# One shared ring of four PSUM banks, and a convolution gate computed in place, in a two-layer hybrid decoder trunk

## The chip, the cores and the metric

The kernel runs on one core of a Trainium2 chip. The metric is the device time of one execution in microseconds (us), the median of several runs. TensorE (PE) multiplies matrices into PSUM; its weight loads (PEld) overlap its matmuls. VectorE (DVE) and ScalarE (ACT) read PSUM and write SBUF, GpSimd (POOL) works on SBUF, and SyncE (SP) issues the DMAs.

## The reference, cut to what matters

There are two layers over 512 tokens of width 1024. Each layer normalises x to h, projects h to the inputs of four mixers and of a gate, and multiplies the mixers' outputs by the gate, projects them back, normalises and adds:

```python
h = rms_norm(x, pre_norm_g[l])
u = h @ w_in[l]                       # mla | sb | moba | conv | gate
o_a = mla_attention(...)              # causal softmax, 4 heads
o_b = stick_breaking_attention(...)   # sigmoids and a running product, 4 heads
o_c = moba_attention(...)             # softmax with a position bias, 4 heads
a, g = split(u_conv)
xg = a * sigmoid(g)                   # 256 channels
y = depthwise causal convolution of xg, 31 taps, + bias
o_d = silu(layer_norm(y)) @ pw_w + pw_b
y = concat(o_a, o_b, o_c, o_d) * silu(u_gate)
x = x + rms_norm(y @ w_out[l], post_norm_g[l])
```

## The kernel before

The instruction order is written by a planner that runs while the kernel is built. Every piece of work is a generator, a task with a priority (`spawn(priority, task)`; a smaller number goes first). A task yields an engine, an estimated duration and the time from which its inputs are there. `run()` keeps an estimated clock for each engine and lets the task go next whose estimated start, plus a weight times its priority, is smallest. Each engine then executes its instructions in that fixed order; what the planner misjudges shows on the chip as a wait. A change of a buffer therefore makes a new plan for the whole program.

Buffers come from rings. `take(tag, ...)` takes a free buffer of a ring or suspends the task until one is given back with `drop`; tasks that wait for the same ring are asked in the order of their priorities. PSUM has eight banks: `acc` 3, `sc` 2 (scores), `tr` 2 (transposes), `pv` 1. Of the SBUF rings, `zb` has two buffers of 513 columns and `cx` two of 542.

- **Filler** (`filler`, priority 300). The projections of h in the order vC, cg, ca, g0, m0, m1, g2, b0, g3, b1, vB, g1, then the output projection. `feat_chunk` (matmuls at L647) makes 2 x 24 matmuls of 128x512 for a chunk of 256 columns; each 24 fill one `acc` bank, which an `evac` task empties with ACT and DVE. Chunk m0 holds q and k of the first two moba heads (`qk_chunk`, evacuation at L809 and L814), g0 to g3 the gate (`gate_chunk`, L840 and L842).
- **Convolution.** `cg_chunk` takes both `zb` buffers and writes sigmoid(g) into them (ACT, L857). `ca_chunk` takes the two `cx` buffers, clears their first 30 columns (POOL, L868) and multiplies a from PSUM by the gate from `zb` into the rest (DVE, L876), which frees `zb`. `taps` then runs 31 DVE instructions for each 128 channels (L895, L899), which accumulate in an `acc` bank that is held for all 31. `conv_norm` comes after.
- **Attention.** For each of 12 heads four `unit_task`s (128 queries each): scores into `sc` (L1038 or L1043), for softmax a DVE instruction from `sc` into a `zb` buffer (L1070), exp and scaling on ACT (L1078, L1083), transposes into `tr` (L1088), and a split of them into two parts (ACT L376, DVE L382). Stick-breaking units take a `zb` buffer too (L1053). The order of the heads is mla, moba, sb. `pv_task` (priority 12) multiplies by v: eight matmuls into the one `pv` bank (L1104), a copy on ACT (L1111), two additions on DVE (L1117).
- **Weights.** `splitter` casts each weight tile on ACT (L358), `low_part` subtracts on DVE or POOL (L363). `either` is the choice of DVE or POOL for such work; it adds a handicap to DVE, 2000 ns while the convolution's first half runs (`busy`), else 300 ns, and 1500 ns at the very beginning.
- `warm_up` issues matmuls into a PSUM bank before the first input is ready (L441).

Of the kernel before, what the change touches and what calls it, by code (L numbers as in the profile page):

```python
# [13 lines left out]
AF = mybir.ActivationFunctionType  # L14
ALU = mybir.AluOpType
# [4 lines left out]
S = 512  # L20
# [3 lines left out]
DEPTH = 2  # L24
# [6 lines left out]
CW = 31  # L31
# [44 lines left out]
FBS = 1  # L76
SPARE0 = 1500.0
PR = {'low': 155, 'hs': 50, 'lat': 50, 'ev': 50, 'vev': 60, 'va': 65, 'cq': 40, 'q': 35, 'cn': -40, 'pw': -5, 'pv': 12, 'ys': 85, 'ye': 70, 'xn': 20, 'xs': 10, 'bd': 10, 'pre': 70, 'u0': 0, 'u1': 0, 'u2': 21, 'u3': 1}
BANKS = {"acc": 3, "sc": 2, "tr": 2, "pv": 1}
ENGINE = {"dvx": "dve", "plm": "pool"}  # L80
PORT = ("dvx", "pool")
WT = {'pe': 0.078, 'dve': 0.691, 'act': 0.0, 'pool': 0.094, 'sp': 0.496}
# [7 lines left out]
class Flow:  # L90
# [19 lines left out]
    def spawn(self, prio, gen):  # L110
        task = [prio, self.n, gen, None]
        self.n += 1
        self.tasks.append(task)
        self.tasks.sort(key=lambda a: a[:2])
        self.resume(task, None)
# [37 lines left out]
    def wait(self, *names):  # L153
        return (yield lambda: max(self.ev[n] for n in names) if all(n in self.ev for n in names) else None)

    def mark(self, name, t):
        self.ev[name] = t
# [17 lines left out]
    def drop(self, buf, t):  # L175
        buf.at = max(buf.at, t)
        buf.uses -= 1
        if buf.uses == 0:
            self.free[buf.tag].append((buf.at, buf.idx))
            if buf.also:  # L180
                self.drop(buf.also, buf.at)


def pe(n):
    return max(107, 3 + n / 2.255)
# [6 lines left out]
def act(n):  # L192
    return 60 + 0.85 * n
# [6 lines left out]
def dve(n):  # L200
    return 69 + 1.04 * n
# [6 lines left out]
def pool(n):  # L208
    return 150 + 2.1 * n
# [3 lines left out]
def trunk(ctx, tc, x, pre_g, w_in, w_sm, vecs, w_out, post_g, rel_bias, consts, onehot, out):  # L213
    nc = tc.nc
    V, A, G, PE = nc.vector, nc.scalar, nc.gpsimd, nc.tensor
    pEng, aEng, vEng, xEng, gEng, mEng, sEng = "pe", "act", "dve", "dvx", "pool", "plm", "sp"
    fl = Flow()
    spawn, wait, mark, drop = fl.spawn, fl.wait, fl.mark, fl.drop
# [12 lines left out]
    for tag, (_, n) in RING.items():  # L231
        fl.free[tag] = [(0.0, i) for i in range(n)]
    for tag, n in BANKS.items():
        fl.free[tag] = [(0.0, i) for i in range(n)]

    def take(tag, name, n=None, dt=F32, uses=1):
        tag, idx, at = yield from fl.slot(*((tag,) if isinstance(tag, str) else tag))
        if tag in BANKS:
            t = ps.tile([P, 512], F32, name=name, tag=f"{tag}{idx}", bufs=1)
        else:  # L240
            t = ap.tile([P, RING[tag][0]], dt, name=name, tag=f"{tag}_{idx}", bufs=1)
        b = Buf(t if n is None else t[:, :n], tag, idx, at)
        b.uses = uses
        return b
# [68 lines left out]
        return r, t  # L313

    def either(n, t):
        busy = any(("cx", l, 0) in fl.ev and ("ca", l, 0) not in fl.ev for l in range(DEPTH))
        e, t = yield [(xEng, dve(n), t, None, None, SPARE0 if ("h", 0, NT - 1) not in fl.ev else SPARE if busy else 300.0), (gEng, pool(n), t, None, None, 0.0)]
        return (V if e == xEng else G), t

# [41 lines left out]
    def low_part(key, i, raw, r3, h, lo, n, t, b):  # L361
        e, t = yield from either(n, t)
        e.tensor_tensor(lo, r3, h.bitcast(F32), ALU.subtract)  # L363
        drop(raw, t)
        units[key, i] = (h, lo, t, b)
# [4 lines left out]
    def weight(key, k):  # L370
        h, lo, t, b = yield from unit(key, k // 2)
        return h[:, k % 2, :], lo[:, k % 2, :], t, b

    def split(dh, dl, src, n, t, eng=None):
        t = yield aEng, act(n), t
        A.copy(dh, src)  # L376
        if eng is gEng:
            e, t = yield from either(n, t)
            e.tensor_tensor(dl, src, dh.bitcast(F32), ALU.subtract)  # L379
        else:  # L380
            t = yield vEng, dve(n), t
            V.tensor_tensor(dl, src, dh.bitcast(F32), ALU.subtract)  # L382
        return t
# [50 lines left out]

    def warm_up():
        z, t = yield lambda: fl.ev.get("z")
        b = yield from take("pv", "warm")
        zb = z.ap.bitcast(BF16)
        while ("h", 0, 0, 0) not in fl.ev or fl.clock[pEng] < fl.ev["h", 0, 0, 0] - 600:
            te = yield pEng, 107 if t > WARM_AT else 213, t  # L440
            PE.matmul(b.ap[:, :256], zb[:, :P], zb[:, P : P + 256], start=True, stop=True)  # L441
            t = te - LAG
        drop(b, te)
        drop(z, te)
# [190 lines left out]
    def feat_chunk(l, c, evac, pre=None):  # L635
        key = (l, c)
        for m in range(2):
            if pre:
                yield from pre(m)
            a = yield from take("acc", "acc")  # L640
            cs = slice(m * P, (m + 1) * P)
            for k in range(KT):
                th = yield from wait(*[("h", l, t, k // 4) for t in range(NT)])
                wh, wl, tw, b = yield from weight(key, k)
                for i, (w, h) in enumerate(((wh, hs[0]), (wh, hs[1]), (wl, hs[0]))):
                    te = yield pEng, pe(S), max(th, tw, a.at)
                    PE.matmul(a.ap, w[:, cs], h[:, k, :], start=k == 0 and i == 0, stop=k == KT - 1 and i == 2)  # L647
                if m == 1:
                    drop(b, te)
            spawn(PR["ev"], evac(m, a, te))  # L650
# [197 lines left out]
    cx, ca, xn = {}, {}, {}  # L848

    def cg_chunk(l):  # L850
        res = []
        for m in range(2):
            res.append((yield from take("zb", f"cg{m}", S)))

        def evac(m, a, te):
            t = yield aEng, act(S), max(te, res[m].at), "sig"
            A.activation(res[m].ap, a.ap, AF.Sigmoid)  # L857
            drop(a, t)
            mark(("cg", l, m), t)

        cx[l, "g"] = res
        yield from feat_chunk(l, "cg", evac)

    def ca_chunk(l):
        for m in range(2):
            b = cx[l, m] = yield from take("cx", f"cx{m}")
            t = yield mEng, 50, b.at
            G.memset(b.ap[:, : CW - 1], 0.0)  # L868
            b.at = t

        def evac(m, a, te):
            b = cx[l, m]
            tg = yield from wait(("cg", l, m))
            g = cx[l, "g"][m]
            t = yield vEng, dve(S), max(te, tg, b.at)
            V.tensor_tensor(b.ap[:, CW - 1 :], a.ap, g.ap, ALU.mult)  # L876
            drop(a, t)
            drop(g, t)
            mark(("cx", l, m), t)

        yield from feat_chunk(l, "ca", evac)
# [113 lines left out]
    def y_split(l, g, hp, pr, yt, ty):  # L995
        ts = yield from wait(("sg", l, g, hp))
        s = sg[l, g][hp]
        cols = slice(pr * 256, pr * 256 + 256)
        e, t = yield from either(256, max(ts, ty))
        e.tensor_tensor(yt.ap, yt.ap, s.ap[:, cols], ALU.mult)  # L1000
        drop(s, t)
        k = 2 * g + hp
        t = yield from split(ys[0][:, k, cols], ys[1][:, k, cols], yt.ap, 256, t, gEng)
        drop(yt, t)
        mark(("y", l, k, pr), t)
# [89 lines left out]
    def pv_task(l, kind, hp, hh, pt, st, yt):  # L1095
        t0 = yield lambda: max(st.values()) if len(st) == NT else None
        vn = VN[kind]
        tv = yield from wait(*[("v", l, vn, j) for j in range(NT)])
        pv = yield from take("pv", "pv")
        v, v4 = vb[l, vn]  # L1100
        te = yield pEng, 1175, max(t0, tv, pv.at)
        for i, j in PVSEQ:
            lhs = v4[:, j, hp * 2 + hh, : (HD if i else P)]
            PE.matmul(pv.ap[: (HD if i else P), j * P :], lhs, pt[i].ap[:, 4 * j * P : (3 * j + NT) * P],  # L1104
                      start=not i and not j, stop=(i, j) == PVSEQ[-1])
        for b in pt:
            drop(b, te)
        drop(v, te)
        ob = yield from take("ob", "ob")
        t = yield aEng, act(S), max(te, ob.at)  # L1110
        A.copy(ob.ap[:HD, :], pv.ap[HD:, :])  # L1111
        for u in range(2):
            c = slice(u * 256, u * 256 + 256)
            if not hh:
                yt.append((yield from take("yt", "yt")))
            t = yield vEng, dve(256), max(t, yt[u].at)
            V.tensor_tensor(yt[u].ap[hh * HD : (hh + 1) * HD, :], pv.ap[:HD, c], ob.ap[:HD, c], ALU.add)  # L1117
            if hh:
                spawn(PR["ys"], y_split(l, GRP[kind], hp, u, yt[u], t))
        drop(pv, t)  # L1120
        drop(ob, t)
# [239 lines left out]
```

## Time and profile before

| | |
|---|---|
| median of 3 runs | 557.99 us (557.28 to 558.27) |
| the profiled execution | 557.85 us |
| its span, first to last instruction | 555.7 us |
| PE / PEld / DVE / ACT / POOL busy | 536.3 / 460.5 / 421.3 / 367.1 / 186.0 us |
| mean granted TensorE clock | 0.999 |

The profile is of one execution. PE's busy time counts a matmul from its start to its modelled end, and matmuls overlap in the pipeline; so "busy" says that something was under way, and PE's idle time is what is left when nothing was.

### The profile page before, as it was taken

What the parts mean: (1) busy time and instruction counts of PE and PEld (TensorE: products, weight loads), DVE (VectorE), ACT (ScalarE), POOL (GpSimd) and SP (SyncE); (2) the same over time, 40 slices, a digit from 0 to 9 for tenths busy, and PEclk for the clock granted to TensorE, in tenths of its full rate; (3) what the DMA queues carried; (4) which work ended last, traced back from release to release, by engine and by line L of the source; (5) the groups of instructions that cost most, each with busy time, mean ns of one, the idle gap of its engine ahead of it and who ended that gap; (6) DMA issues with size and microseconds to landing.
All of it is one profiled execution on the core that took longest, in us unless ns stands there. A gap on an engine that the chain in (4) does not pass through costs nothing.

```text
span 555.7 us, 9439 instructions
## 1 busy us (share of the span) xinstructions
PE 536.3 (97%) x3181; PEld 460.5 (83%) x3181; DVE 421.3 (76%) x942; ACT 367.1 (66%) x864; POOL 186.0 (33%) x227
## 2 busy tenths in 40 slices
PE   9999999999989999999998999999998999999995
PEld 5997877778868898899998887777876778989995
DVE  4668658999999988953776584999999889697243
ACT  5637568958995746745673665897879558475531
POOL 5733031352224731522332003145323433242321
PEclk9999999999999999999999999999999999999999
DMA  7424233134303163033753214132431322513145
GB/s 279 148 73 140 79 113 97 43 96 128 111 9 114 58 199 105 21 114 128 247 183 99 77 33 138 42 110 67 120 101 58 97 74 60 186 42 96 50 168 181
DMA packets 31026, 59.47 MB, mean 107 GB/s; under 512 B 4034, under 2 KB 5954, under 8 KB 30979
## 3 DMA queue, kind: packets, MB, share of 16 engines
q1 hardware_dynamic: 30978, 58.88, 34.4%
q8 instruction: 25, 0.41, 0.3%
q14 instruction: 23, 0.18, 0.1%
HBM read 49.17 MB, written 5.51 MB: 98 GB/s over the span
## 4 chain that ended last, share of the span: by engine, by line
PE 78%; DVE 10%; ACT 9%; issue 2%; POOL 0%; POOLq 0%; DVEq 0%; ACTq 0%
PE acc L647 31%; PE acc L1132 16%; PE acc L580 7%; PE lat L580 4%; PE pv L1104 4%; PE tr L1088 3%; PE sc L1043 3%; PE sc L1038 2%; ACT p L1083 2%; ACT p L1078 2%; PE acc L710 2%; ACT pt L376 1%; DVE cs L1061 1%; DVE pt L382 1%; PE tr L537 1%
## 5 line engine op out<-in xcount | busy, mean ns | idle before, releaser
L647 PE MATMUL acc<-hH,w 128*128 128x512 f32 x640 | 217.3, 404 | 3.1 <-DVE m L814 1.6
L363 POOL TENSOR_TENSOR w<-raw,w 128x512 fp32r<-128x512 f32 x70 | 94.9, 1361 | 182.1 <-ACT w L358 163.9
L647 PEld LDWEIGHTS acc<-hH,w 128*128 128x128 f32 x640 | 118.5, 188 | 28.2 <-issue 4.0
L647 PE MATMUL acc<-hL,w 128*128 128x512 f32 x320 | 130.0, 406 | 0.0
L358 ACT CAST w<-raw 128x512 fp32r<-128x512 f32 x130 | 79.7, 619 | 44.2 <-PE acc L647 18.3
L899 DVE SCALAR_TENSOR_TENSOR cv<-cx,vec,cv 128x512 f32<-128x512 f32 x116 | 86.6, 747 | 1.2
L1132 PE MATMUL acc<-w,yH 128*128 128x256 f32 x416 | 75.4, 282 | 0.0
L647 PEld LDWEIGHTS acc<-hL,w 128*128 128x128 f32 x320 | 60.3, 188 | 11.5 <-issue 0.9
L363 DVE TENSOR_TENSOR w<-raw,w 128x512 fp32r<-128x512 f32 x60 | 41.4, 697 | 34.6 <-ACT w L358 34.3
L1132 PEld LDWEIGHTS acc<-w,yH 128*128 128x128 f32 x416 | 64.5, 189 | 0.2
L1132 PE MATMUL acc<-w,yL 128*128 128x256 f32 x208 | 58.9, 283 | 0.1
L580 PE MATMUL acc<-w,hH 128*128 128x256 f32 x256 | 49.0, 286 | 0.3 <-DVE w L363 0.3
L382 DVE TENSOR_TENSOR pt<-tr,pt 128x128 fp32r<-128x128 f32 (+3 forms) x96 | 45.8, 483 | 4.0 <-ACT pt L376 3.3
L1088 PE MATMUL tr<-cst,p 128*128 128x128 f32 x240 | 42.5, 275 | 5.8 <-ACT p L1083 5.6
L376 ACT CAST pt<-tr 128x128 fp32r<-128x128 f32 (+3 forms) x96 | 40.3, 423 | 11.3 <-PE tr L1088 10.4
L1088 PEld LDWEIGHTS tr<-cst,p 128*128 128x128 f32 x240 | 29.9, 141 | 19.3 <-ACT p L1083 10.9
L580 PEld LDWEIGHTS acc<-w,hH 128*128 128x128 f32 x256 | 40.3, 189 | 1.1 <-DVE w L363 0.5
L1132 PEld LDWEIGHTS acc<-w,yL 128*128 128x128 f32 x208 | 39.2, 189 | 0.3 <-DVE yL L379 0.3
L580 PE MATMUL acc<-w,hL 128*128 128x256 f32 x128 | 36.2, 283 | 0.0
L1078 ACT ACTIVATE p<-zb,s 128x128 f32<-128x128 f32 (+2 forms) x64 | 35.8, 560 | 0.5 <-ACT p L1083 0.3
L1083 ACT ACTIVATE p<-p,s 128x128 f32<-128x128 f32 (+3 forms) x64 | 35.0, 561 | 0.4 <-DVE s L1081 0.4
L1063 POOL TENSOR_TENSOR p<-p,cs 128x128 f32<-128x128 f32 (+3 forms) x22 | 18.3, 836 | 43.7 <-DVE cs L1061 24.2
(176 smaller groups left out, 1021.9 us busy)
## 6 DMA issues: line engine op xcount, KB each, us to landing
raw<-in_w_in_dram SPq DMA_DIRECT2D x96, 256.0 KB, 2.7
raw<-in_w_out_dram SPq DMA_DIRECT2D x32, 256.0 KB, 2.6
xt<-in_x_dram SPq DMA_DIRECT2D x8, 512.0 KB, 4.1
raw<-in_w_sm_dram SPq DMA_DIRECT2D x8, 256.0 KB, 3.8
bias<-scratch SPq DMA_DIRECT2D x8, 256.0 KB, 3.1
m<-m SPq DMA_DIRECT2D x16, 128.0 KB, 2.2
b<-b SPq DMA_DIRECT2D x16, 128.0 KB, 3.0
x<-xt SPq DMA_DIRECT2D x4, 512.0 KB, 2.9
```

Source lines behind the costliest of these rows:

```text
L358: A.copy(wH, r3)
L363: e.tensor_tensor(lo, r3, h.bitcast(F32), ALU.subtract)
L376: A.copy(dh, src)
L382: V.tensor_tensor(dl, src, dh.bitcast(F32), ALU.subtract)
L580: PE.matmul(o, a[:, k, tc_], w, start=k == 0 and i == 0, stop=k == KT - 1 and i == 2)
L647: PE.matmul(a.ap, w[:, cs], h[:, k, :], start=k == 0 and i == 0, stop=k == KT - 1 and i == 2)
L899: V.scalar_tensor_tensor(o.ap if j == CW - 1 else a.ap, xc[:, j : j + S], vc[:, w0 : w0 + 1], a.ap, ALU.mult, ALU.add)
L1078: A.activation(p.ap[:, :wd], src.ap[:, :wd], AF.Exp, bias=nm[:, 0:1], scale=-1.0, accum_out=ls)
L1083: A.activation(p.ap[:, :wd], p.ap[:, :wd], AF.Copy, scale=r[:, 0:1])
L1088: PE.transpose(tr3[:, j, :], p.ap[:, j * P : (j + 1) * P], ident)
L1104: PE.matmul(pv.ap[: (HD if i else P), j * P :], lhs, pt[i].ap[:, 4 * j * P : (3 * j + NT) * P], start=not i and not j, stop=(i, j) == PVSE ...
L1132: PE.matmul(o, a[:, k, tc_], w, start=first and i == 0, stop=stop and i == 2)
```

## The change

The `pv` bank is given up and `acc` has four banks; `pv_task` and `warm_up` take theirs from `acc`. `cg_chunk` takes the `cx` buffers instead of `zb`, clears their first columns and writes the sigmoid into the rest; `ca_chunk` multiplies in place. `either` keeps the high handicap until the second half of the convolution is done.

```diff
-BANKS = {"acc": 3, "sc": 2, "tr": 2, "pv": 1}
+BANKS = {"acc": 4, "sc": 2, "tr": 2}
@@ either
-        busy = any(("cx", l, 0) in fl.ev and ("ca", l, 0) not in fl.ev for l in range(DEPTH))
+        busy = any(("cx", l, 0) in fl.ev and ("ca", l, 1) not in fl.ev for l in range(DEPTH))
@@ warm_up
-        b = yield from take("pv", "warm")
+        b = yield from take("acc", "warm")
@@ cg_chunk
-        res = []
-        for m in range(2):
-            res.append((yield from take("zb", f"cg{m}", S)))
-
-        def evac(m, a, te):
-            t = yield aEng, act(S), max(te, res[m].at), "sig"
-            A.activation(res[m].ap, a.ap, AF.Sigmoid)
-            drop(a, t)
-            mark(("cg", l, m), t)
-
-        cx[l, "g"] = res
-        yield from feat_chunk(l, "cg", evac)
-
-    def ca_chunk(l):
         for m in range(2):
             b = cx[l, m] = yield from take("cx", f"cx{m}")
             t = yield mEng, 50, b.at
@@
         def evac(m, a, te):
             b = cx[l, m]
+            t = yield aEng, act(S), max(te, b.at), "sig"
+            A.activation(b.ap[:, CW - 1 :], a.ap, AF.Sigmoid)
+            drop(a, t)
+            mark(("cg", l, m), t)
+
+        yield from feat_chunk(l, "cg", evac)
+
+    def ca_chunk(l):
+        def evac(m, a, te):
+            x_ = cx[l, m].ap[:, CW - 1 :]
             tg = yield from wait(("cg", l, m))
-            g = cx[l, "g"][m]
-            t = yield vEng, dve(S), max(te, tg, b.at)
-            V.tensor_tensor(b.ap[:, CW - 1 :], a.ap, g.ap, ALU.mult)
+            t = yield vEng, dve(S), max(te, tg)
+            V.tensor_tensor(x_, a.ap, x_, ALU.mult)
             drop(a, t)
-            drop(g, t)
             mark(("cx", l, m), t)
@@ pv_task
-        pv = yield from take("pv", "pv")
+        pv = yield from take("acc", "pv")
```

## Rows read from the trace of the kernel before

**Rows 1.** The page: span, and busy time, and busy tenths in 40 equal slices.
```profile
span 555.7 us, 9439 instructions
PE 536.3 (97%) x3181; PEld 460.5 (83%) x3181; DVE 421.3 (76%) x942; ACT 367.1 (66%) x864; POOL 186.0 (33%) x227
...
PE   9999999999989999999998999999998999999995
...
DVE  4668658999999988953776584999999889697243
ACT  5637568958995746745673665897879558475531
PEclk9999999999999999999999999999999999999999
```

**Rows 2.** Windows: stretch, length, busy us (count) of each engine, clock, DMA, GB/s.
```profile
97.00:126.00 29.00, 27.44 (x137) 21.79 (x136) 27.14 (x59) 22.22 (x52) 13.40 (x14) 1.00 0.26 76
126.00:181.00 55.00, 52.74 (x272) 42.74 (x271) 51.29 (x128) 45.68 (x108) 18.76 (x23) 1.00 0.31 87
368.00:394.00 26.00, 25.27 (x127) 20.46 (x125) 24.05 (x51) 19.71 (x40) 13.64 (x15) 1.00 0.29 82
394.00:440.00 46.00, 41.63 (x214) 33.24 (x213) 43.71 (x107) 39.29 (x93) 15.62 (x16) 1.00 0.28 81
46.00:72.00 26.00, 25.43 (x117) 20.36 (x115) 17.88 (x27) 14.06 (x25) 3.18 (x5) 1.00 0.39 117
```

**Rows 3.** Windows around four stalls of PE, the same columns.
```profile
108.00:112.00 4.00, 2.44 (x17) 1.99 (x16) 3.74 (x7) 3.92 (x7) 0.74 (x1) 1.00 0.00 0
155.00:163.00 8.00, 5.74 (x33) 4.04 (x32) 7.42 (x19) 7.91 (x19) 1.57 (x3) 1.00 0.00 1
404.00:415.00 11.00, 10.00 (x56) 7.89 (x55) 9.92 (x21) 8.11 (x16) 2.57 (x2) 1.00 0.40 109
424.00:433.00 9.00, 5.63 (x33) 4.10 (x32) 8.55 (x17) 8.85 (x18) 1.18 (x1) 1.00 0.10 29
```

**Rows 4.** The chain, 156 to 163 and 429 to 433: start, us, what.
```profile
157.74 0.48 ACT b L809
...
159.84 1.32 PE pv L1104 x8
...
162.85 1.17 PE acc L647 x5
...
429.96 0.68 DVE b L814
...
431.26 0.70 DVE b L814
...
432.10 0.93 PE acc L647 x3
```

**Rows 5.** Timeline around the first scores and the first unit of each layer.
```profile
51.22 0.82 PE L1038 MATMUL sc<-kT,qT 96*128 96x128 f32 x4
71.27 0.69 DVE L876 TENSOR_TENSOR cx<-acc,cg 128x512 f32<-128x512 f32 x1 [2.30 <-PE acc L647]
72.00 0.29 DVE L1070 CUSTOM_DVE_ANT_0 zb<-sc,mask 128x128 f32<-128x128 f32 x1
322.05 0.82 PE L1038 MATMUL sc<-kT,qT 96*128 96x128 f32 x4
340.24 0.29 DVE L1070 CUSTOM_DVE_ANT_0 zb<-sc,mask 128x128 f32<-128x128 f32 x1
```

**Rows 6.** Windows in which those scores stand, the columns of Rows 2.
```profile
51.00:72.00 21.00, 20.44 (x96) 16.57 (x94) 14.09 (x21) 10.23 (x18) 1.67 (x3) 1.00 0.33 101
322.00:340.00 18.00, 18.00 (x81) 14.50 (x82) 12.78 (x21) 9.25 (x16) 0.00 (x0) 1.00 0.29 85
```

**Rows 7.** Chain: projections without a pause; timeline of ACT around one table load.
```profile
59.21 14.11 PE acc L647 x61
...
115.68 10.62 PE acc L647 x46
...
382.36 9.97 PE acc L647 x43
430.45 1.28 ACT L840 ACT_TABLE_LOAD   x1
431.74 0.60 ACT L840 ACTIVATE sg<-acc 128x512 f32<-128x512 f32 x1
```

**Rows 8.** Lines, second half of the convolution in layer 0: the choice of engine.
```profile
L363 DVE TENSOR_TENSOR w<-raw,w 128x512 fp32r<-128x512 f32 x2 | 1.4, 692 | 0.0
L363 POOL TENSOR_TENSOR w<-raw,w 128x512 fp32r<-128x512 f32 x10 | 12.9, 1291 | 25.8 <-ACT w L358 24.1 <-DVE sg L842 1.7
```

## The prediction

> **What bounds the kernel.** I read the page first, then the windows, then the chain of waits, then the timeline. The page shows PE under way in nearly every slice, at the full granted clock (the 2.4 GHz level), while DVE and ACT are full only in parts [rows 1]. The change removes no matmul. So its gain can come only from time in which PE has nothing under way, and that time is small: 555.7 minus 536.3 us busy is 19.4 us [rows 1], and part of it is the kernel's beginning and end, which no edit here touches.
>
> Where is the rest? The windows give it by stage [rows 2]: length minus PE's busy time is 1.56 us in 97 to 126, 2.26 in 126 to 181, 0.73 in 368 to 394, 4.37 in 394 to 440 and 0.57 in 46 to 72. That is 9.5 us, and I take it as the most that the change can give. These are the stretches in which the convolution's taps run beside attention, and in the first four DVE is 92 to 95% busy.
>
> Four short windows hold nearly all of it [rows 3]: 1.56 us near 110, 2.26 near 159, 1.00 near 409, 3.37 near 429, together 8.2 us. In three of them ACT is full too (3.92 of 4, 7.91 of 8, 8.85 of 9 us). The chain says what PE wanted there [rows 4]: a bank. In the last one, the two DVE instructions that empty a bank of chunk b (L814, the second ends at 431.96) are followed 0.14 us later by the next projection matmuls. Near 159 the same chunk's evacuation (L809 at 157.74) stands in the chain, PE does only transposes and a product with v, and projections resume just before 162.85. One of the three `acc` banks belongs to the taps for this whole time, so the projections alternate between two, and an evacuation that is late by more than the 24 matmuls of the other bank stops them. A matmul of L647 takes 14.11/61 = 0.231 us [rows 7], so that is 24 x 0.231 = 5.55 us.
>
> **The fourth bank.** Outside the product with v, a free fourth bank would carry the projections through each of those stalls: 5.55 us of work against at most 3.37 us of stall. But the same bank is what the product with v used, and eight matmuls of L1104 stand inside such a stall [rows 4]. If pv_task, which has the smaller priority number, gets the bank, the projections have two as before and nothing is gained; if the filler, which asks as soon as it has issued a chunk, gets it first, the stall is covered and the product waits for the next evacuation while PE has other work. So the two ends are 0 and 8.2 us, and no row tells who asks first. I take the middle, **4.1 us**. A loss from this edit is possible where the product with v then comes late and nothing else is left for PE; that is in the third rival.
>
> **The gate in place.** The number and the shapes of the instructions are the same: two memsets, two sigmoids and two multiplications per layer; the multiplication reads its second operand from `cx` instead of `zb`, with the same 512 columns, 0.69 us [rows 5]. I cost that at nothing. It would be hidden in any case: PE's projections run through it without a pause. The memsets move from ahead of chunk ca to ahead of chunk cg; POOL is busy 1.67 of 21 us there [rows 6], and nothing queues behind them. No DMA moves with them.
>
> What changes is who holds `zb`. Before, the scores of the first mla units are ready at 52.0 us (51.22 + 0.82), and the DVE instruction that empties them starts at 72.00, 0.04 us after the multiplication that frees the gate's buffer (71.27 + 0.69); in layer 1 it is 322.9 and 340.24 [rows 5]. So attention stands still for 20.0 and 17.4 us for want of a `zb` buffer, and the change lets it start at once. This does not shorten the chain by that much. PE is under way 20.44 of 21 and 18.00 of 18 us in those windows [rows 6], so a transpose or a score that moves in pushes a projection out, and the time is conserved. The moba heads also wait for chunk m0, which stands behind the same sum of PE work. What moves for nothing is DVE and ACT work, into time in which they are free: DVE has 6.9 and 5.2 us there, ACT 10.8 and 8.8 us [rows 6]. The 12.1 us of DVE then fall out of the crowded stretches, in which DVE's idle time is 1.86 + 3.71 + 1.95 + 2.29 = 9.8 us [rows 2]. That makes late evacuations rarer. Its worth in PE time lies between nothing and the 1.3 us of stalls that the fourth bank does not reach (9.5 minus 8.2); I take 0, since new interleaving can also cost, below.
>
> **ACT's tables.** exp and sigmoid sit in different tables, and a switch is a load of 1.28 us, after which the next instruction starts 0.01 us later [rows 7]. Before, both sigmoids of cg precede the first exp in each layer; with units running early, each may need a switch there and back: at most 2 x 2 per layer, 8 loads, 10.3 us of ACT. In the two windows ACT has 10.8 and 8.8 us free [rows 6], so at 5.1 us per layer they fit and I cost them at nothing; without that cover each costs up to 1.28 us, since a bank of the ring waits behind it.
> The Trainium skill, ScalarE: Activation LUTs, section What ACT_TABLE_LOAD costs, speaks harder against the change: it adds a drain of about 1.38 us to every load, about 2.66 us a switch. By it, as an estimate, eight switches would be 21.3 us, more than ACT has free in the two windows together. The rows of this trace do not show such a drain.
>
> **The handicap in `either`.** In the second half of the convolution of layer 0, two of twelve weight subtractions went to DVE, 1.4 us; the others are on POOL already at 1.29 us each [rows 8]. The edit can move those and a few like them. POOL is busy 18.76 of 55 us there [rows 2], so it is hidden; what it frees on DVE is 1.4 us, against a POOL instruction that is 0.6 us longer. Cost and gain 0.
>
> **The warm-up's bank.** It holds one of four banks until the first tile is ready, so three remain, as before. 0.
>
> **The sum.** 557.85 minus 4.1 is **553.8 us**; the profiled execution is 0.14 us under the median of the three runs, so I leave the sum as it is. A difference of 0.2%, 1.1 us, is about what a measurement of this kernel can tell from none.
>
> **Rivals.** First, all stalls go: filler gets the bank each time, and less crowded DVE and ACT remove the rest. 557.85 - 9.5 = 548.3 us. For it: 5.55 us of cover against stalls of 3.4 us or less. Against: products with v inside the stalls. Chance 0.13.
>
> Second, nothing comes of it: DVE and ACT are the limit in those 156 us, a bank more only moves the wait to the next evacuation or to the transposes, and the new plan has its own misjudgements. 557.9 us, within 1.1. For it: ACT full in three of the four windows [rows 3]. Chance 0.16.
>
> Third, slower, by one mechanism: units that start early put transposes among the projections of cg and ca. PE executes in order, so every exp that is late stops it, where now 61 projections follow each other without a pause [rows 7]. In the mixed stretches PE idles 8.9 of 156 us, 5.7% [rows 2]; over the 39 us of the two windows that is 2.2 us, and a table load for which PE waits adds 1.28 us. Without a gain from the bank the time is 560.1, with one load 561.3. With the gain of 4.1 us the mechanism decides from the second waited load on: 2.2 + 2 x 1.28 = 4.8. The product with v that waits for a bank behind an evacuation would add to the same exp-to-transpose chain. For it: the planner's order was made for the old buffers, and every misjudged duration becomes a wait on PE. Against: projections run without attention between them after 115 and after 382 us too, 46 and 43 in a row [rows 7], so the early units may only change places with them. Chance 0.26.
>
> **How the numbers follow.** The forecast has 0.45, with its own range from 549.7 (8.2 us gone) to 556.7 (1.1 us). Faster is 0.45 + 0.13 = 0.58, same 0.16, slower 0.26. The range reaches from 547.5, a little below the first rival, to 561.3, the third with one waited load; beyond it lie two or more waited loads or a plan better or worse than any of these, which I give 2 in 10.
>
> **What would show each step.** In the changed profile: the first L1070 within 2 us of the first scores in both layers; DVE and ACT busier between 51 and 72 us and less so later; up to eight more table loads; PE's idle time beside the taps down from 8.9 us to about 5, and no projection that waits for L814. PE's busy time and instruction counts, the weight loads' total, and the tail stay. The prediction is wrong if PE waits on exp between 50 and 75 us, if the products with v wait for a bank while PE is idle, or if the plan after the convolution leaves PE waiting for the last heads before the output projection.

## The result and the profile after

The changed kernel takes 550.54 us (median of 4 runs, 550.13 to 550.59) against 558.06 us before (4 runs, 557.28 to 558.27). The ratio is 0.9866, with a 95% interval of 0.9849 to 0.9883: 7.5 us faster, where 4.1 us were forecast. The profiled execution took 550.13 us. Two executions, one of the kernel before and the profiled one of e9 (747.1 us at a granted clock of 0.659), were slow ones; they are left out of every time given here, and e9 has no stages to read.

The page of the changed kernel (span; busy us, share and instructions of each engine; busy tenths in 40 slices):
```profile
span 548.4 us, 9464 instructions
PE 533.1 (97%) x3181; PEld 462.3 (84%) x3181; DVE 412.0 (75%) x920; ACT 364.6 (66%) x864; POOL 212.0 (39%) x249
...
DVE  3667875879999978953875598577899998798243
ACT  5638997349994736656664699944699656574531
```
Against [rows 1], PE has the same 3181 matmuls. Its idle time, span minus busy, falls from 19.4 to 15.3 us. DVE has 22 instructions less and POOL 22 more. ACT is full in slices 5 and 6, where it had been half full, and emptier in slices 7 and 8.

The windows of the changed kernel that answer to [rows 2] and [rows 6] (same columns):
```profile
97.00:126.00 29.00, 29.00 (x131) 23.77 (x130) 23.67 (x37) 13.11 (x23) 17.06 (x17) 1.00 0.36 100
126.00:181.00 55.00, 53.66 (x278) 44.16 (x277) 51.86 (x125) 47.25 (x116) 26.24 (x32) 1.00 0.34 96
368.00:394.00 26.00, 26.00 (x118) 21.26 (x117) 21.08 (x33) 12.98 (x24) 18.17 (x18) 1.00 0.41 112
394.00:440.00 46.00, 44.81 (x234) 36.62 (x233) 43.36 (x108) 40.27 (x97) 19.78 (x22) 1.00 0.35 98
51.00:72.00 21.00, 20.45 (x97) 14.88 (x96) 17.92 (x52) 20.10 (x51) 6.31 (x5) 1.00 0.18 51
```
PE's idle time in the four stretches beside the taps falls from 8.9 us to 0 + 1.34 + 0 + 1.19 = 2.5 us. From 51 to 72 us ACT goes from 10.23 to 20.10 us and DVE from 14.09 to 17.92, and PE's idle time there stays at 0.55 us (0.56 before). From 97 to 126 us ACT falls from 22.22 to 13.11 us.

What PE waited for (us in total, times, longest), three lines of the kernel before and then two of the changed kernel, in which L1111 is the old L1117:
```profile
PE tr L1088 <- ACT p L1083: 5.6, 6, 1.7
PE acc L647 <- DVE m L814: 1.6, 1, 1.6
PE acc L647 <- DVE b L814: 1.2, 1, 1.2
```
```profile
PE acc L647 <- DVE yt L1111: 1.3, 1, 1.3
PE pv L1098 <- DVE sg L842: 1.1, 1, 1.1
```
Before, the longest wait was not for a bank: transposes waited 5.6 us for the scaled exp on ACT, and projections 2.8 us for their own banks. Both kinds are gone in the changed kernel. In their place a projection waits 1.3 us for a bank that a product with v holds, and a product with v waits 1.1 us, near 430 us, behind the evacuation of a gate chunk while PE is idle. The prediction had named the last as a sign of being wrong.

The timeline of DVE at the first units, then of ACT at the gate's sigmoids (start, us, engine, line):
```profile
51.58 0.28 DVE L1064 CUSTOM_DVE_ANT_0 zb<-sc,mask 128x128 f32<-128x128 f32 x1
...
317.03 0.28 DVE L1064 CUSTOM_DVE_ANT_0 zb<-sc,mask 128x128 f32<-128x128 f32 x1
```
```profile
52.43 1.28 ACT L1072 ACT_TABLE_LOAD   x1
78.52 1.28 ACT L860 ACT_TABLE_LOAD   x1
79.81 0.60 ACT L860 ACTIVATE cx<-acc 128x512 f32<-128x512 f32 x1
81.37 0.59 ACT L860 ACTIVATE cx<-acc 128x512 f32<-128x512 f32 x1
```
The first unit starts at 51.58 instead of 72.00 us, in layer 1 at 317.03 instead of 340.24 [rows 5]. The plan puts both sigmoids of cg behind the mla units, at 79.81 and 81.37 us, so one load of their table serves both. The next instruction follows a load by 0.01 to 0.02 us here too; the drain that the Trainium skill (ScalarE: Activation LUTs, What ACT_TABLE_LOAD costs) adds does not show.

### The profile page after: what moved, and what is told of

Same layout as the page of the kernel before. It is cut to its first block, busy times and chain, and to the rows that moved or that the text cites. A ratio compares the mean times of both kernels' runs of the same rounds, so it can differ in the third digit from the quotient of the medians.

```text
span 548.4 us, 9464 instructions
## 1 busy us (share of the span) xinstructions
PE 533.1 (97%) x3181; PEld 462.3 (84%) x3181; DVE 412.0 (75%) x920; ACT 364.6 (66%) x864; POOL 212.0 (39%) x249
## 4 chain that ended last, share of the span: by engine, by line
PE 86%; DVE 8%; ACT 3%; issue 2%; POOL 0%; POOLq 0%; DVEq 0%; ACTq 0%
PE acc L647 36%; PE acc L1126 15%; PE acc L580 8%; PE lat L580 5%; PE pv L1098 5%; PE tr L1082 4%; PE sc L1037 3%; PE sc L1032 2%; DVE cs L1055 1%; PE tr L537 1%; PE warm L441 1%; PE acc L710 1%; DVE kT L783 1%; PE acc L968 1%; PE gb L486 1%
## 5 line engine op out<-in xcount | busy, mean ns | idle before, releaser
L647 PE MATMUL acc<-hH,w 128*128 128x512 f32 x640 | 212.0, 403 | 1.4 <-DVE yt L1111 1.3
L363 POOL TENSOR_TENSOR w<-raw,w 128x512 fp32r<-128x512 f32 x81 | 107.3, 1332 | 153.4 <-ACT w L358 140.0
L647 PEld LDWEIGHTS acc<-hH,w 128*128 128x128 f32 x640 | 118.2, 188 | 26.2 <-ACT ob L1105 1.7
L647 PE MATMUL acc<-hL,w 128*128 128x512 f32 x320 | 129.4, 404 | 0.0
L1126 PE MATMUL acc<-w,yH 128*128 128x256 f32 x416 | 75.7, 282 | 0.0
L647 PEld LDWEIGHTS acc<-hL,w 128*128 128x128 f32 x320 | 60.2, 188 | 11.8
L1126 PEld LDWEIGHTS acc<-w,yH 128*128 128x128 f32 x416 | 64.5, 189 | 0.3
L1126 PE MATMUL acc<-w,yL 128*128 128x256 f32 x208 | 58.7, 282 | 0.0
L363 DVE TENSOR_TENSOR w<-raw,w 128x512 fp32r<-128x512 f32 x49 | 35.5, 731 | 26.0 <-ACT w L358 25.6
L580 PE MATMUL acc<-w,hH 128*128 128x256 f32 x256 | 49.0, 285 | 1.9 <-DVE w L363 1.9
L1082 PE MATMUL tr<-cst,p 128*128 128x128 f32 x240 | 41.1, 273 | 1.7 <-DVE pt L382 1.2
L580 PEld LDWEIGHTS acc<-w,hH 128*128 128x128 f32 x256 | 40.1, 189 | 2.6 <-DVE w L363 2.1
L1126 PEld LDWEIGHTS acc<-w,yL 128*128 128x128 f32 x208 | 39.2, 189 | 0.0
L580 PE MATMUL acc<-w,hL 128*128 128x256 f32 x128 | 36.5, 285 | 0.0
L1077 ACT ACTIVATE p<-p,s 128x512 f32<-128x512 f32 (+3 forms) x64 | 34.8, 561 | 1.4 <-DVE s L1075 1.3
L1057 POOL TENSOR_TENSOR p<-p,cs 128x128 f32<-128x128 f32 (+3 forms) x25 | 21.5, 873 | 31.9 <-DVE cs L1055 20.6
```

The source lines that it names most:

```text
L580: PE.matmul(o, a[:, k, tc_], w, start=k == 0 and i == 0, stop=k == KT - 1 and i == 2)
L1077: A.activation(p.ap[:, :wd], p.ap[:, :wd], AF.Copy, scale=r[:, 0:1])
L1082: PE.transpose(tr3[:, j, :], p.ap[:, j * P : (j + 1) * P], ident)
L1126: PE.matmul(o, a[:, k, tc_], w, start=first and i == 0, stop=stop and i == 2)
```

## The experiments

Two questions stood: which edit brings the gain, and how much of it is the plan itself, since every edit makes the planner order the whole program anew. Times are medians; each run is compared with runs of the kernel before on the same chip.

**The parts, one plan each.** e1_bank is the change of `BANKS`, `warm_up` and `pv_task` alone:
```diff
-BANKS = {"acc": 3, "sc": 2, "tr": 2, "pv": 1}
+BANKS = {"acc": 4, "sc": 2, "tr": 2}
-        b = yield from take("pv", "warm")
+        b = yield from take("acc", "warm")
-        pv = yield from take("pv", "pv")
+        pv = yield from take("acc", "pv")
```


> Only the fourth acc bank shared with the product with v; the gate stays in zb and the handicap as before. Theory of the prediction (the bank carries the projections through the stalls): 553.9 us, 4.1 us under before, and PE's idle time beside the taps falls from 8.9 to about 5 us; no projection waits for L814. Rival, the gate in place does it: within 1 us of 558. Rival, every new plan differs by chance: anything within 3 us of 558, with no relation to the sum of the parts.

Measured: 558.48 us, ratio 0.9998 (0.9980 to 1.0016). The waits of PE in e1_bank (us in total, times, longest):
```profile
PE acc L647 <- DVE yt L1117: 4.1, 2, 3.2
PE pv L1104 <- DVE yt L1117: 2.4, 1, 2.4
PE acc L580 <- DVE w L363: 1.9, 1, 1.9
PE acc L647 <- DVE b L814: 1.2, 1, 1.2
```
L1117 is the last reader of a product with v. Before, transposes waited 5.6 us for ACT and projections 2.8 us for their own evacuations. In e1 the wait for ACT is gone and 1.2 us of L814 stay, but projections wait 4.1 us for a bank that a product with v holds, and a product waits 2.4 us for another's. The stall has changed its owner.

e2_inplace is the new `cg_chunk` and `ca_chunk` alone, with `BANKS`, `warm_up`, `pv_task` and `either` as before:
```diff
@@ cg_chunk
-            res.append((yield from take("zb", f"cg{m}", S)))
...
+            b = cx[l, m] = yield from take("cx", f"cx{m}")
...
-            A.activation(res[m].ap, a.ap, AF.Sigmoid)
+            A.activation(b.ap[:, CW - 1 :], a.ap, AF.Sigmoid)
@@ ca_chunk
-            V.tensor_tensor(b.ap[:, CW - 1 :], a.ap, g.ap, ALU.mult)
+            V.tensor_tensor(x_, a.ap, x_, ALU.mult)
```

> Only the gate in place (cx instead of zb); acc 3 and pv 1 as before, handicap as before. Theory of the prediction: the first units start 20 and 17 us earlier and the time stays within 1.5 us of 558, since PE is full there and the stalls for banks remain. Rival, the early start relieves ACT and DVE where projections stall: 551 to 553 us, and the stalls near 110, 159 and 430 us are gone without another bank.

Measured: 559.75 us, ratio 1.0029 (1.0016 to 1.0042), 1.7 us slower, a little beyond the 1.5 us that were expected; the rival is out.

e3_either is the handicap alone:
```diff
-        busy = any(("cx", l, 0) in fl.ev and ("ca", l, 0) not in fl.ev for l in range(DEPTH))
+        busy = any(("cx", l, 0) in fl.ev and ("ca", l, 1) not in fl.ev for l in range(DEPTH))
```


> Only the handicap of DVE kept through the second half of the convolution. Theory of the prediction: a few subtractions go from DVE to POOL, within 1.1 us of 558. Rival, DVE is the limit in the second half and each subtraction there costs PE time: 2 us faster. Rival, chance of the plan: up to 3 us either way.

Measured: 556.87 us, ratio 0.998 (0.9961 to 0.9998), 1.2 us faster, about the least that can be told from no change and just over the 1.1 us of the expectation.

e4_bank_inplace is the whole change without that line of `either`.

> The bank and the gate in place, without the change of the handicap. Theory of the prediction: as the whole change, 550.5 us within 1.1. If the handicap matters: 552 us or more. If bank and gate add up, the difference to before is the sum of those of e1_bank and e2_inplace.

Measured: 557.15 us, ratio 0.9988 (0.9971 to 1.0005). Parts of +0.4, +1.7 and -1.2 us stand against a whole of -7.5, and the one line of `either` makes 6.6 us of it. That is either an interplay of the edits or the luck of a plan, so the next runs drew other plans.

**Other plans.** One number of the planner that the hardware never sees, the delay that it assumes from one engine to the next, was moved by a few nanoseconds:
```diff
-LAG = 330
+LAG = 335
```
(329 in e6.) e5 and e6 are the whole change, e7 the kernel before, e8 the whole change without the handicap's line.

> The whole change; one constant of the planner that means nothing to the hardware, the delay from one engine to the next, is 335 ns instead of 330, so that the plan is a different draw. Theory A (the three edits work together: the gate in place makes the taps late, the handicap brings them back, the bank lets the projections run ahead): 550.5 within 2 us. Theory B (the gain is a lucky plan): 555 to 559 us, no different from the partial changes.

> The whole change with the planner's delay at 329 ns, another draw of the plan. Theory A: 550.5 within 2 us. Theory B: 555 to 559 us.

> The kernel before with the planner's delay at 335 ns. Tells how far the plan alone moves the kernel before. Theory A: within 2 us of 558. Theory B: the draws of before spread as widely as those of after, by 3 us or more, and may reach 554.

> Bank and gate in place without the handicap's change, with the planner's delay at 335 ns, to be compared with e5. Theory A: about as without the delay's change, 557 us, and 5 us or more over e5, with the taps ending later than in e5. Theory B: as e5 within the spread of the draws.

Measured: e5 544.44 us, ratio 0.9738 (0.9715 to 0.9761); e6 557.99, 0.9977 (0.9959 to 0.9994); e7 553.14, 0.9897 (0.9871 to 0.9923); e8 549.87, 0.9833 (0.9807 to 0.9858). The whole change spreads over 13.5 us in three draws and the kernel before over 4.9 us in two, so both theories were too simple. But at one and the same constant the order is kept: before, without the handicap, whole are 558.1, 557.2, 550.5 at 330 ns and 553.1, 549.9, 544.4 at 335 ns. The whole change gives 7.5 and 8.7 us, the handicap's line 6.6 and 5.4 us of it. At 329 ns, where the whole change takes as long as the kernel before does at 330, the kernel before was not timed. e5 is the fastest of all kernels of this study, 14.1 us under the kernel before.

**Bank and gate alone in the second draw, and the taps brought forward another way.** e9 and e10 are e1 and e2 with `LAG = 335`. e11 and e12 are e4 and e8 with
```diff
-TAP_EARLY = 100
+TAP_EARLY = 40
```
which lets the taps go earlier on DVE without the handicap.

> Only the bank, with the planner's delay at 335 ns, to be compared with the kernel before at 335 ns (553.1). Theory P (bank and gate gain only together: alone, the product with v holds the fourth bank just when the projections want it): 553 within 2.5 us, and PE's idle time from 97 to 181 us stays at 3 us or more. Theory S (each edit has its own gain and e1_bank was an unlucky plan): 548 to 551 us and under 2.5 us of idle there.

> Only the gate in place, with the planner's delay at 335 ns. Theory P: 553 to 556 us, stalls for banks remain in 97 to 181 and 330 to 430 us, taps end near 192 us. Theory S: 548 to 551 us.

> Bank and gate without the handicap's change, but the planner's weight of the taps is 40 in place of 100 as long as they are not late, so that they go earlier on DVE. Theory T (late taps cost e4_bank_inplace its gain at the ends of the layers): the taps end by 186 and 452 us as in the whole change, and the time is 549 to 553 us against 557.2. Rival (the handicap matters by what it moves to POOL, or the plan's chance): taps earlier, time 555 us or more.

> As e11 with the planner's delay at 335 ns, to be compared with e8_nohandicap_lag335 (549.9) and e5_after_lag335 (544.4). Theory T: 544 to 547 us. Rival: 549 us or more, attention now waits behind the taps on DVE.

Measured: e9 548.20 us (three executions), ratio 0.9827 (0.9803 to 0.985); e10 554.43, 0.9945 (0.9928 to 0.9961); e11 555.97, 0.9977 (0.9959 to 0.9995); e12 551.24, 0.9887 (0.9863 to 0.9911). The bank alone is thus worth +0.4 us in one draw and -4.9 in the other, against theory P; e10 came as theory P had it. The gate alone costs 1.7 and 1.3 us. These four runs were on another chip; each set against the kernel before on its own chip, e9 is 3.9 us faster than e7 and e10 2.7 us slower. At 330 ns bank and gate together (e4, -0.9 us) are 3.0 us better than their sum (+2.1); at 335 ns they are about the sum (e8 -3.3 us, sum -3.6). So no joint effect shows in the times of the second draw. Theory T falls with e11 and e12.

All six kernels that were timed at both constants are faster at 335 ns, by 4.7 to 10.3 us (the bank alone most, the kernel before by 4.9). So the constant moves them in common, which speaks for comparing at equal constants. But by that range the worth of an edit can still differ by some 5 us from draw to draw (an estimate). The bank's own worth does, and one or two pairs don't settle a smaller effect.

**Where the time is, by stage.** Length minus PE's busy time, worked out from the windows of each kernel. "Beside taps" is 100 to 200 plus 330 to 430 us, "ends" the output stages, 200 to 260 plus 430 to 530 us, "boundary" 260 to 330 us:
```
                              us   beside taps   ends   boundary
before                     558.1       7.9        1.9      1.8
bank (e1)                  558.5       7.8        2.6      2.3
gate (e2)                  559.8       6.3        4.9      1.8
handicap (e3)              556.9       7.5        1.1      1.8
bank, gate (e4)            557.2       2.0        7.8      3.2
bank, gate, taps (e11)     556.0       4.0        3.0      3.1
whole                      550.5       2.9        1.4      3.2
whole, 329 ns (e6)         558.0       2.9        5.1      3.6
before, 335 ns (e7)        553.1       8.0        0.8      0.6
gate, 335 ns (e10)         554.4       6.7        2.0      0.6
bank, gate, 335 ns (e8)    549.9       3.5        2.9      0.0
bank, gate, taps 335 (e12) 551.2       4.0        3.6      0.0
whole, 335 ns (e5)         544.4       2.4        0.8      0.0
```
The times are medians, the stages those of one profiled execution, which lay up to 1.8 us from its median (e1 556.69, e4 558.77, e6 556.42 us). The stretches are fixed in time, so a faster kernel has later work in each: from 430 to 530 us 600 matmuls in e4, 661 in the changed kernel.

Three things can be read from it. Beside the taps the idle time is, in every row (the bank alone at 335 ns has none), 7.5 us or more without the gate, 6.3 or more with the gate alone, and 4.0 or less with bank and gate. At the ends the handicap lowers it at equal constants: from 1.9 to 1.1 without the other edits, from 7.8 to 1.4 and from 2.9 to 0.8 with them; but e6 has 5.1 with the handicap, so it is no guarantee. The boundary goes with the draw more than with the edits: 0 to 0.6 at 335 ns, 1.8 to 3.6 else.

The table leaves out what TensorE's clock did. In the changed kernel PE idles 1.87 us at the boundary until 290.45 us, where it waits for a weight (L363 on DVE). From 291.25 us on the granted clock is 0.50, the 1.2 GHz level, until 294.66 (the clock stands behind POOL's column):
```profile
286.00:291.25 5.25, 2.91 (x23) 2.53 (x22) 4.92 (x13) 3.69 (x12) 1.15 (x2) 1.00 0.37 144
291.25:294.66 3.41, 3.41 (x13) 3.41 (x13) 2.33 (x4) 0.00 (x0) 0.23 (x1) 0.50 0.79 234
```
The 128x352 matmuls of L580 start every 0.29 us there and every 0.16 us after it, so about 1.5 us are lost (an estimate, 3.41 x (1 - 0.16/0.29)), and they count as busy. e5 has neither this wait nor this stretch: the boundary's 3.2 us idle and these 1.5 us are 4.7 of the 5.9 us between the two profiled executions. Such a stretch stands once in e1, e3, e4, e6, e8, e10, e11 and e12 and twice in e2, each close behind 1.7 to 3.2 us in which PE idled; the kernel before, e5 and e7 have none between their first 12 and their last 5 us. It doesn't follow each time: e3 falls behind a wait of 1.68 us near 427 us, and the kernel before doesn't behind the same wait, 1.70 us.

The windows behind three of those rows, first e4_bank_inplace, then the changed kernel, then e5 (stretch, length, busy us of PE, PEld, DVE, ACT, POOL):
```profile
100.00:200.00 100.00, 98.02 (x508) 81.54 (x507) 90.55 (x188) 70.05 (x157) 45.69 (x52) 1.00 0.37 102
430.00:530.00 100.00, 93.50 (x600) 81.89 (x599) 76.94 (x145) 57.01 (x133) 34.99 (x51) 1.00 0.30 86
```
```profile
100.00:200.00 100.00, 98.07 (x510) 81.70 (x509) 89.66 (x189) 70.06 (x159) 52.57 (x58) 1.00 0.36 101
430.00:530.00 100.00, 98.61 (x661) 89.39 (x662) 73.02 (x143) 57.69 (x139) 40.73 (x54) 1.00 0.31 96
```
```profile
260.00:330.00 70.00, 69.99 (x471) 64.30 (x470) 52.42 (x130) 49.02 (x136) 22.02 (x25) 1.00 0.41 129
430.00:530.00 100.00, 99.17 (x687) 90.69 (x686) 70.92 (x139) 55.67 (x134) 39.38 (x53) 1.00 0.31 96
```
From 100 to 200 us e4 and the changed kernel are alike on PE; they part at the ends. The waits of PE from 430 to 530 us in e4:
```profile
PE acc L1126 <- DVE yL L379: 2.0, 2, 1.5
PE tr L1082 <- DVE p L1057: 1.7, 1, 1.7
PE sc L1037 <- ACT p L1051: 1.4, 2, 0.9
PE pv L1098 <- DVE sg L842: 1.2, 1, 1.2
```
The output projection (L1126) and the last heads' scores and transposes wait for work on DVE and ACT that comes late. The last taps of e4 and of the changed kernel, as rows of tile cv (count, ns min/median/max, first and last start):
```profile
L893 DVE SCALAR_TENSOR_TENSOR ca<-cx,vec,cv x4: 737/748/749, 136.3 to 464.9; 128x512 f32<-128x512 f32 x4
```
```profile
L893 DVE SCALAR_TENSOR_TENSOR ca<-cx,vec,cv x4: 740/748/749, 135.8 to 451.0; 128x512 f32<-128x512 f32 x4
```
The taps end near 466 us in e4 and near 452 in the changed kernel. Part of what stood between them is in the lines of e4, 137.8 to 193.9 us:
```profile
L1057 DVE TENSOR_TENSOR p<-p,cs 128x512 f32<-128x512 f32 (+1 forms) x3 | 2.6, 874 | 0.0
L363 DVE TENSOR_TENSOR w<-raw,w 128x512 fp32r<-128x512 f32 x2 | 1.4, 683 | 0.0
```
In that half of the convolution the changed kernel has none of either on DVE. Counted over all that `either` places, it is 7 in e4 in each layer's second half, 10.2 us of DVE in both layers, 7 and 8 in e8 (8.8 us), 5 and 1 in the kernel before (3.3 us), and none in e3 or in the three draws of the whole change.

Bringing the taps forward did not do the same. In e11 the last tap ends near 451 us as in the whole change, and the ends recover from 7.8 to 3.0 us, but the idle time beside the taps goes from 2.0 to 4.0: from 100 to 200 us PE waits 1.8 us for the normalisation behind the convolution (L929) and 0.8 us for ACT (L1077), which it does not in e4. In e11 only 3 of those instructions (1.5 us) are left on DVE in the two second halves, and in e12 2 (1.1 us), and still they take 5.4 and 6.8 us longer than the whole change. So neither the end of the taps nor an emptier DVE in the second half is enough for the gain. The changed kernel also has 9 instructions more on POOL than e11 (249 against 240) and 4.9 us less of DVE (412.0 against 416.9); that this is what counts is not shown.

## Why the prediction was right, step by step

The direction and the range held; the size, 4.1 us, was a little over half of what was measured, and the terms behind it were in part the wrong ones. That the time fell where it was forecast is in part luck: in two other plans the same change takes 544.4 us, below the whole range, and 558.0 us, no gain over the kernel before at 330 ns.

- **What bounds the kernel.** Right in that PE's matmuls are the same, and only its waiting changed. Idle time makes up 4.1 us of the 7.3 us of the span (19.4 to 15.3); the rest lies in PE's busy time, 536.3 to 533.1 us. A matmul of L647 counts as busy for about 0.39 us, while the next one starts 0.231 us after it [rows 7], so a shorter wait stays inside the busy time. As an estimate, the time from start to start of neighbouring matmuls, above the tenth percentile for the same two shapes and without idle time, sums to 34.6 us before and 31.8 in the changed kernel, and beside the taps to 15.3 and 10.2. The prediction left this out of the 9.5 us that it took as the most. At equal constants the gain stayed below that (7.5 and 8.7 us). One of its stretches, 46 to 72 us, lies ahead of the first tap at 80.1 us.
- **"The fourth bank", 4.1 us.** The doubt was right and the term is not settled. The chain was read as showing that PE wanted a bank in the four windows; by the waits it was a bank for 2.8 us of the 8.2 (L814), and for 4.8 us transposes waited for ACT (L1083), with no projection between them. Alone, the bank gave +0.4 and -4.9 us in two draws, and e1 shows the case that was priced at nothing: the product with v holds the bank. Who comes first, the filler or pv_task, is decided by the plan.
- **"The gate in place", 0.** The mechanism is right: the first units start at once, ACT and DVE work moves from 97 to 126 us into 51 to 72 us, and PE pays nothing there. Alone it is a loss of 1.7 and 1.3 us. The mla units now go ahead of chunk ca: in the changed kernel the first multiplication of the gate starts at 86.64 us, where a multiplication stood at 71.27 [rows 5], and the first tap moves from 80.1 to 94.8. In e2 the last taps end near 192 and 460 us instead of 181 and 440. That this lateness makes the loss is not shown; e2 also has two stretches at the lower clock. Neither it nor a joint effect was in the sum: bank and gate together take the idle time beside the taps from 7.9 to 2.0 us (e4), which neither does alone at 330 ns. At 335 ns (8.0 to 3.5, e8) the bank alone has no stages, and its time of 548.2 us is below that of both, 549.9. The prediction took the relief of DVE and ACT as worth 0 to 1.3 us, and counted it apart from the bank.
- **"The handicap in `either`", cost and gain 0.** This step failed. Alone it is small, 1.2 us, about as forecast. But the prediction priced it in the plan of before, where 2 of 12 subtractions were on DVE in the second half [rows 8], 5 and 1 instructions in the two layers over all that `either` places; with bank and gate it was 7 and 7 (e4) or 7 and 8 (e8). Added last, it is worth 6.6 and 5.4 us there, the largest step in both draws. How it gains that much stays open, since e11 and e12 have nearly as few of these instructions on DVE and not the gain.
- **"ACT's tables", 0.** Right, and even the bound was far: 17 loads before and after, because the plan holds both sigmoids of cg back behind the units.
- **"The warm-up's bank", 0.** Not tested by itself; PE's idle time up to 50 us is 1.33 us before and 1.28 after.
- **The third rival**, transposes that stop PE among the projections of cg and ca, did not come: 0.56 and 0.55 us idle from 51 to 72 us. Its side remark, a product with v that waits for a bank, did, with 1.1 us.
- **The second rival** had a point that the runs make stronger: "the new plan has its own misjudgements". At 329 ns the whole change takes 558.0 us, as the kernel before. The boundary's 3.2 us in the changed kernel is such a misjudgement; at 335 ns it is gone.

What stays open: how the bank's term and the gate's share the gain beside the taps, by what way the handicap gains, and how the mean over many plans would come out. Two pairs at equal constants give 7.5 and 8.7 us; the third draw of the whole change has no partner. So the gain is shown for these two pairs of plans, and its cause in part only argued.

## What to carry to other kernels

Where a planner or a scheduler orders the program, one time is one draw: move a constant that means nothing by 1% and time both kernels again before an edit is credited, and compare at equal constants. Price an edit in the plan that the other edits make; a handicap that was worth 1.2 us alone made 6.6 and 5.4 us once the other two edits were in. A pooled buffer can leave a wait where its two users want it at the same moment, as in e1: look for the wait under the other user's name.

## What was not expected of the hardware

The stretches at the 1.2 GHz level in the middle of kernels that PE fills to 97%: a mean granted clock of 0.996 hides one, and behind a wait of PE it adds about 1.5 us that no idle time shows. The other surprise is the plan's part: 5 ns in an assumed delay moved the kernel before by 4.9 us and the changed kernel by 6.1 us, nearly as much as the edits.
